# Softmax of 33.55 MB on one core: ten loads and thirteen stores of mixed size become eight and eight of 16 rows per partition

## Chip, cores, metric

One core of a Trainium2 chip; the other cores are idle. The metric is the device time of one launch in microseconds (us), median over several runs. The profile's span is about 1.9 us shorter than the time. The ratios compare runs in the fast state alone; the granted clock is 1.0.

## The reference

```python
x = np.random.randn(16, 1024, 512).astype(np.float32)      # 16,384 rows of 512
x_max = np.max(x, axis=-1, keepdims=True)
exp_x = np.exp(x - x_max)
return exp_x / np.sum(exp_x, axis=-1, keepdims=True)
```

33.55 MB are read and 33.55 MB written.

## The kernel before

The rows are cut into chunks. A chunk of R rows per partition is one load (128 x R x 2 KB), is worked on in place in groups of at most 8 rows, and is stored from the same place. The program's buffer in SBUF holds 96 rows per partition, so the last chunks take the place of the first ones and wait for those stores.

```python
CHUNKS = [                      # (rows per partition, first row in SBUF)
    (3, 0), (5, 3), (8, 8), (16, 16), (16, 32), (16, 48), (16, 64), (16, 80), (16, 0), (16, 16),
]
EARLY = 8                       # loads issued at once
AFTER_STORE = {2: [8], 3: [9]}  # load 8 after the store of chunk 2, ...
GROUP = 8
FINISH_BEFORE = (1, 2, 3)       # finish the waiting group before these chunks are begun
STORE_ROWS = {3: 8, 4: 8, 5: 8} # these chunks are stored in halves of 8 rows
ON_VECTOR = 3                   # the last three groups are scaled on VectorE
AT_HEAD = {mybir.EngineType.SP: 3}   # three loads go ahead of the entry barrier
...
def rowmax(g):   # VectorE: minus the maximum of 8 rows, one instruction
def exps(g):     # ScalarE: per row exp(x + shift), with its sum
def scale(g):    # VectorE reciprocal; GpSimd multiplies 8 rows (or VectorE, row by row)
    ...
    if since is not None:
        nc.scalar.dma_start(out=dst[k][:, since:b, :], in_=place[k][:, since:b, :])
    if b == CHUNKS[k][0]:
        for later in AFTER_STORE.get(k, ()):
            load(later)
...
for k in range(EARLY):
    load(k)                     # nc.sync.dma_start
for g, (k, a, _, _) in enumerate(groups):
    if waiting is not None and a == 0 and k in FINISH_BEFORE:
        scale(waiting); waiting = None
    rowmax(g); exps(g)
    if waiting is not None:
        scale(waiting)
    waiting = g
scale(waiting)
```

Loads are issued from SyncE, stores from ScalarE: two queues on the same 16 DMA engines.

## Time and profile before

| | before |
|---|---|
| time, median of 6 runs beside the changed kernel | 161.51 us (161.40 to 161.61) |
| span of the profiled run | 159.6 us |
| DMA packets of data per engine (packet records) | 184 |

The part of the profile that the prediction does not show is the list of DMA issues: out<-in, the issuing queue, how many, KB each, and the median time in us from issue to landing.

```profile
held<-in_x_dram SPq DMA_DIRECT2D x7, 4096.0 KB, 39.1
out_dram<-held ACTq DMA_DIRECT2D x4, 4096.0 KB, 29.1
out_dram<-held ACTq DMA_DIRECT2D x7, 2048.0 KB, 37.9
held<-in_x_dram SPq DMA_DIRECT2D x1, 768.0 KB, 4.4
out_dram<-held ACTq DMA_DIRECT2D x1, 768.0 KB, 15.8
```

The first load of 768 KB lands after 4.4 us; later a load of 4 MB, which takes 9.7 us when alone, lands 39 us after its issue (the median). A transfer that lands late here is mostly one that was queued early.

"Packet records" below are the trace's rows of single DMA packets: queue, start, duration, size. A packet is what one partition moves in one transfer (16 rows: 32 KB). The page prints only their sums; the numbers from them are worked out here, and say so. The records don't name the DMA engine; it follows from the times, since each packet starts where another of the same engine ends.

### The profile page before, as it was taken

To read this page: it belongs to the slowest core of one execution; us is meant where nothing else is said; L and a number is where in the kernel's file an instruction comes from. 1 tells how busy PE (TensorE), PEld (TensorE's weight loads), DVE (VectorE), ACT (ScalarE), POOL (GpSimd) and SP (SyncE) were. 2 spreads that over 40 slices of the span, in tenths; PEclk is the share of its full clock that TensorE was granted. 3 is DMA by queue.
4 is the path that set the end of the run, shared out by engine and by line. 5 is a ranking of instruction groups with operands and counts; after the bars stand their busy time and mean duration, and the time that the engine had idled before them with its cause. 6 is when DMAs were issued, how large, how long until landed. Compare 5 with 4: busy or idle time off the path is not lost.

```text
span 159.6 us, 442 instructions
## 1 busy us (share of the span) xinstructions
DVE 82.6 (52%) x58; ACT 92.9 (58%) x257; POOL 91.2 (57%) x18
## 2 busy tenths in 40 slices
DVE  0470903980966567393856768386479935000000
ACT  0719076039949796976979957993995760000000
POOL 0060912950899999999999999999930000000000
DMA  7999999999999999999999999989999999999994
GB/s 271 439 464 398 431 391 435 458 408 421 431 423 431 427 415 443 411 468 423 431 456 411 437 423 431 464 378 448 406 468 443 445 411 419 476 411 419 468 419 172
DMA packets 3315, 67.13 MB, mean 421 GB/s; under 512 B 368, under 2 KB 368, under 8 KB 624
## 3 DMA queue, kind: packets, MB, share of 16 engines
q1 hardware_dynamic: 1440, 33.56, 49.6%
q10 hardware_dynamic: 1872, 33.56, 49.0%
q14 instruction: 3, 0.02, 0.0%
HBM read 33.55 MB, written 33.55 MB: 420 GB/s over the span
## 4 chain that ended last, share of the span: by engine, by line
POOL 51%; issue 12%; ACT 11%; DVE 7%; DMA 3%; ACTq 0%; DVEq 0%; POOLq 0%
POOL held L150 51%; ACT held L135 11%; DVE held L157 4%; DMA held<-in_x_dram 3%; DVE shift L127 3%; ACTq L163 0%; DVE recip L147 0%; DVEq L209 0%; POOLq L150 0%; DVEq L147 0%; ACTq L135 0%
## 5 line engine op out<-in xcount | busy, mean ns | idle before, releaser
L135 ACT ACTIVATE held<-held,shift 128x512 f32<-128x512 f32 x128 | 90.4, 708 | 33.0 <-POOL held L150 29.9
L150 POOL TENSOR_TENSOR held<-held,recip 128x4096 f32<-128x4096 f32 (+2 forms) x14 | 91.0, 6529 | 25.8 <-DVE recip L147 25.8
L127 DVE TENSOR_REDUCE shift<-held 128x8 f32<-128x4096 f32 (+2 forms) x17 | 70.3, 4139 | 5.4 <-DMA held<-in_x_dram 5.4
L147 DVE RECIPROCAL recip<-sums 128x8 f32<-128x8 f32 (+2 forms) x17 | 3.4, 200 | 45.9 <-ACT held L135 45.9
L135 ACT ACTIVATION_READ_ACCUMULATOR held<-held,shift 128x1 f32 x128 | 24.0, 187 | 0.0
L157 DVE TENSOR_SCALAR held<-held,recip 128x512 f32<-128x512 f32 x24 | 10.0, 491 | 0.1
L135 ACT ACT_TABLE_LOAD x1 | 1.3, 1283 | 4.5 <-DMA held<-in_x_dram 4.5
L198 POOL MEMSET const-float32-0.0<- 128x1 f32 x1 | 0.1, 98 | 0.2 <-issue 0.2
L198 POOL MEMSET const-bfloat16-1.0<- 128x1 bf16 x1 | 0.1, 101 | 0.0
L198 POOL MEMSET const-uint8-127<- 128x1 uint8 x1 | 0.1, 101 | 0.0
L198 POOL MEMSET const-float32-1.0<- 128x1 f32 x1 | 0.1, 98 | 0.0
## 6 DMA issues: line engine op xcount, KB each, us to landing
held<-in_x_dram SPq DMA_DIRECT2D x7, 4096.0 KB, 39.1
out_dram<-held ACTq DMA_DIRECT2D x4, 4096.0 KB, 29.1
out_dram<-held ACTq DMA_DIRECT2D x7, 2048.0 KB, 37.9
held<-in_x_dram SPq DMA_DIRECT2D x1, 2048.0 KB, 11.5
held<-in_x_dram SPq DMA_DIRECT2D x1, 1280.0 KB, 7.1
out_dram<-held ACTq DMA_DIRECT2D x1, 1280.0 KB, 20.5
held<-in_x_dram SPq DMA_DIRECT2D x1, 768.0 KB, 4.4
out_dram<-held ACTq DMA_DIRECT2D x1, 768.0 KB, 15.8
```

The lines of the kernel that those rows point to most:

```text
L127: nc.vector.reduce_max(out=shift[g], in_=place[k][:, a:b, :], axis=AX, negate=True)
L135: nc.scalar.activation(out=place[k][:, r, :], in_=place[k][:, r, :], func=EXP, bias=shift[g][:, r - a : r - a + 1], scale=1.0, accum_out=s ...
L147: nc.vector.reciprocal(out=recip, in_=sums[g])
L150: nc.gpsimd.tensor_tensor(out=place[k][:, a:b, :], in0=place[k][:, a:b, :], in1=recip.unsqueeze(2).to_broadcast([P, b - a, d]), op=mybir.A ...
L157: nc.vector.tensor_scalar_mul(out=place[k][:, r, :], in0=place[k][:, r, :], scalar1=recip[:, r - a : r - a + 1],)
L198: nc = _bacc.Bacc("TRN2", target_bir_lowering=False, num_devices=1)
```

## The change

Its intent: fewer and larger transfers, all alike; no small ones at the opening nor in mid kernel.

```diff
-CHUNKS = [
-    (3, 0), (5, 3), (8, 8), (16, 16), (16, 32), (16, 48), (16, 64), (16, 80), (16, 0), (16, 16),
-]
+CHUNKS = [(16, 0), (16, 16), (16, 32), (16, 48), (16, 64), (16, 80), (16, 0), (16, 16)]
-EARLY = 8
-AFTER_STORE = {2: [8], 3: [9]}
+EARLY = 6
+AFTER_STORE = {0: [6], 1: [7]}
-FINISH_BEFORE = (1, 2, 3)
+FINISH_BEFORE = ()
-STORE_ROWS = {3: 8, 4: 8, 5: 8}
+STORE_ROWS = {}
```

## The prediction

> **What bounds the kernel now.** I read the page from the top: the engines' shares, then the DMA rows of the slices, then the DMA queues, then a table of stretches, and only then the chain and the groups.
>
> ```profile
> span 159.6 us, 442 instructions
> DVE 82.6 (52%) x58; ACT 92.9 (58%) x257; POOL 91.2 (57%) x18
> DMA  7999999999999999999999999989999999999994
> GB/s 271 439 464 398 431 391 435 458 408 421 431 423 431 427 415 443 411 468 423 431 456 411 437 423 431 464 378 448 406 468 443 445 411 419 476 411 419 468 419 172
> DMA packets 3315, 67.13 MB, mean 421 GB/s; under 512 B 368, under 2 KB 368, under 8 KB 624
> q1 hardware_dynamic: 1440, 33.56, 49.6%
> q10 hardware_dynamic: 1872, 33.56, 49.0%
> ```
>
> No compute engine is busy for more than 58% of the span. The 16 DMA engines are: the DMA row is 9 everywhere but in the first and the last slice, and the loads (q1) and stores (q10) together fill 49.6 + 49.0 = 98.6% of the engines' time. The 67.1 MB are fixed by the task (33.55 in, 33.55 out). So the time is the bytes over the rate, plus the ends. The stretches show where the rate is less than it can be:
>
> ```profile
> 0.00:2.00 2.00, 0.00 (x0) 0.00 (x0) 0.20 (x4) 1.00 0.48 135
> 2.00:12.00 10.00, 4.64 (x3) 3.52 (x8) 2.75 (x1) 1.00 1.05 445
> 12.00:22.00 10.00, 4.48 (x2) 4.77 (x13) 4.46 (x1) 1.00 0.99 405
> 22.00:32.00 10.00, 5.38 (x3) 4.59 (x14) 5.09 (x1) 1.00 1.02 436
> 32.00:42.00 10.00, 5.26 (x3) 7.60 (x21) 3.46 (x2) 1.00 1.01 422
> 42.00:106.00 64.00, 42.25 (x19) 53.21 (x151) 64.00 (x10) 1.00 1.00 430
> 108.00:157.00 49.00, 19.50 (x30) 17.23 (x50) 9.21 (x2) 1.00 1.01 434
> 157.00:159.60 2.60, 0.00 (x0) 0.00 (x0) 0.00 (x0) 1.00 0.12 50
> ```
>
> The last two columns are DMA share and GB/s; a packet is counted whole where it starts or ends, so short stretches swing by some per cent. Stores alone (108 to 157) run at 434 GB/s, the mix (42 to 106) at 430, and the only stretches below are the first 2 us and those from 12 to 42 us, at 405 and 422, with the DMA share still 0.99 and 1.01: there packets are slow, not absent. The chain and the groups:
>
> ```profile
> POOL 51%; issue 12%; ACT 11%; DVE 7%; DMA 3%; ACTq 0%; DVEq 0%; POOLq 0%
> ...
> 131.60 2.38 DVE held L157 x6
> ```
>
> ```profile
> L135 ACT ACTIVATE held<-held,shift 128x512 f32<-128x512 f32 x128 | 90.4, 708 | 33.0 <-POOL held L150 29.9 <-DVE shift L127 3.0
> L150 POOL TENSOR_TENSOR held<-held,recip 128x4096 f32<-128x4096 f32 x12 | 83.8, 7017 | 13.1 <-DVE recip L147 13.1
> L127 DVE TENSOR_REDUCE shift<-held 128x8 f32<-128x4096 f32 x15 | 65.7, 4388 | 1.0 <-DMA held<-in_x_dram 1.0
> ```
>
> The chain gives POOL 51% of the span, which misleads: it follows instructions, and its last one ends at 134.0 us, 25 us before the span does. Those 25 us are stores still queued. POOL's cadence is a margin to be checked, not the bound.
>
> **What the Trainium skill says.** (1) "DMA: Bandwidth & Descriptors", section "Where 436 GB/s comes from", puts the ceiling of the 16 engines at 435.2 GB/s. The trace agrees: 434 with stores alone. (2) The same page, section "Queues, rings and completion order", says that an engine takes turns between its queue rows, one packet at a time. The trace agrees: between 44 and 48 us, with load packets of 32 KB and store packets of 16 KB, the packet records give 282 GB/s of loads and 150 of stores, about 2 to 1. (3) The same page, section "Why small descriptors are slow (HBM only)", names a fixed cost per packet. The packet records agree: the usual packet of 6,144 bytes takes 234 ns, 16,384 take 611 and 32,768 take 1,213; a line through the first and last has an intercept of 8 ns and 27.2 bytes per ns, and gives 610 ns for the middle one. (4) "Perfetto Trace Analysis", [...]says that splitting transfers can help where DMA engines are generally idle. Here they are not, so I expect the opening's small transfers to buy no bandwidth.
>
> **The change part by part.** Ten loads (3, 5, 8 and seven of 16 rows) become eight of 16; thirteen stores (3, 5, 8, six of 8 rows and four of 16) become eight of 16. All loads but the last two are issued at once; load 6 waits for store 0, load 7 for store 1. Compute is the same per row but for two POOL calls fewer. What follows is an estimate from the durations above.
>
> *Fixed cost.* Each engine moves 8 packets per transfer: 80 + 104 = 184 packets before, 64 + 64 = 128 after. 56 packets at 8 ns are 0.45 us, and 7 completion descriptors of 9 ns are 0.06: **0.5 us gained**, on the path, as every engine is full.
>
> *The slow stretches.* The packet records between 12 and 42 us hold some 90 load packets that take 25 to 320 ns over 1,213, all of 32 KB, while store packets of 6, 10 and 16 KB come in between; summed and divided by 16 engines this is 0.8 us. After 42 us there is hardly one. I can't tell whether the small stores cause it, which go, or the 32 KB loads themselves early on, which stay. I count half: **0.4 us gained**.
>
> *Opening.* First bytes move at 1.0 us in both, since the first load is issued at 0.0. The first packets of before carry 0.3 us per engine above their size; with 32 KB packets I allow **0.1 us more**. What the small first load bought, the first reduction at 4.4 us, is gone: the first 4.19 MB land at about 12.3 us (in before the three small loads, the same bytes: issued at 0.9 and 11.5 to landing).
>
> *Does DMA go idle later?* From 12.3: reduce to 16.7 and 21.1 (4.39 each), exponentials of 8 rows 5.7 each to 22.5 and 28.2, POOL 7.0 each to 29.8 and 36.8, so store 0 is issued at 36.9, where before had sent three. Until then loads fill the engines alone, and six loads last for 25.2 / 0.431 = 58 us. Its first packet follows some 2 to 3 us later (before: issued 11.5, first packet 15.2), about 39, when 16 MB are in. From then on packets are equal and each queue gets 216 GB/s, 19.4 us per transfer. Stores 0 to 3 land at 59, 78, 98, 117; loads 4 to 7 at 62, 81, 101, 120. Load 6 is released at 59 and not due until 81; load 7 at 78 and 101: 22 us to spare each. Stores are issued at 51, 65, 79 and 93 (two POOL calls, 13.95 apart in before's chain), faster than 19.4, so the store queue never runs dry in between.
>
> *The end.* Load 7 lands at about 121. At 120, 17.5 of 33.55 MB are stored; the queue holds the rest of store 4 and store 5 (issued about 113.5, as the reciprocal of its second half stands behind the reduction that waits for load 6), 7.6 MB or 17.5 us: dry at 137.5. Store 6 stands behind the reduction of load 7's first half: 121 + 4.4 + 0.2 + 3.5 of scaling = 129, after exponentials 132: 5.5 us spare. Store 7: the second reduction ends near 133, exponentials 139, reciprocal and scaling 3.5, so 143, and the queue is dry at 147: 4 us spare. So the DMA engines stay full and the last transfer is again 4 MB.
>
> Sum: -0.5 - 0.4 + 0.1 = -0.8: 161.5 - 0.8 = **160.7 us**.
>
> **Rivals.** (a) *The late start costs.* If the kernel were bound by compute, first arithmetic 7.9 us later (12.3 for 4.4) and POOL's later start would push the end by up to 8 us: 165 to 170. For it: the chain is POOL; against: the DMA row of 9s and the 25 us of queued stores at the end. (b) *Store 6 or 7 comes late.* My spare is 4 to 5.5 us at the end, the smallest of the schedule; if loads 6 and 7 land later than at equal shares, each us beyond the spare is added: 162 to 164. Against: in before, loads land as the shares say. (c) *The slow load packets are of the opening with 32 KB loads*, and a longer time of loads alone makes more of them: at 415 GB/s instead of 431 for 37 us, 1.4 us lost: 162. For it: all slow packets are 32 KB loads; against: 22 to 26 us, nearly loads alone, ran at 430. (d) *All slow packets go*: another 0.4 gained, 160.3, the least that I see, since 67.1 MB at 433 are 155.0 us, and with 1.0 ahead, 0.5 for first packets, 1.0 behind and the 1.9 us between span and time, 159.4 is the floor.
>
> **Range and chances.** Between (d) and (c): 160.1 to 162.1. Faster by 2% would be 158.3, below that floor: 0.01. Slower by 2% would be 164.7 and needs (a) or a failed (b): 0.04. Within 2%: 0.95.
>
> **What would show it.** DMA row of 9s throughout, with the first store at about 37 us; packets down by about 1,000; load 6 issued near 59, load 7 near 78; last load landing at 120 instead of 109; last DVE scaling at about 143 instead of 134; DVE's and ACT's idle at the start up by 8 us without moving the end. A wrong prediction shows as a slice below 9 near 137 or 147 us (b), a low GB/s with full share before 40 us (c), or DMA idle before 59 us (a load that waits where I see none).

## The result

| | before | after |
|---|---|---|
| time, median of 6 | 161.51 us | 161.90 us (161.74 to 162.38) |
| span of the profiled run | 159.6 us | 159.9 us |
| ratio of fast runs, 95% interval | | 1.0028 (1.0013 to 1.0044) |

A ratio is the mean time of one kernel's fast runs over that of the other's of the same rounds, so not quite the ratio of the medians. By the 2% rule the two are the same; the difference of 0.4 us is small but outside the noise, and it has the other sign than forecast.

The same parts of the page after:

```profile
span 159.9 us, 418 instructions
DVE 82.0 (51%) x56; ACT 92.7 (58%) x257; POOL 91.0 (57%) x17
DMA  7999999999899999999999999999999999999994
GB/s 270 459 451 393 459 451 402 434 467 410 338 410 426 426 451 402 418 484 402 418 484 410 418 467 420 393 443 475 393 418 492 402 418 477 410 410 443 451 410 189
DMA packets 2307, 67.13 MB, mean 420 GB/s; under 512 B 256, under 2 KB 256, under 8 KB 256
q1 hardware_dynamic: 1152, 33.55, 49.6%
q10 hardware_dynamic: 1152, 33.55, 48.7%
```

A thousand records fewer, and the DMA engines are as full as before. In the GB/s row one slice stands out: the eleventh, 40 to 44 us, at 338. The stretches (the last two columns are DMA share and GB/s):

```profile
0.00:2.00 2.00, 0.00 (x0) 0.00 (x0) 0.20 (x4) 1.00 0.90 262
22.00:32.00 10.00, 8.36 (x4) 10.00 (x29) 9.22 (x2) 1.00 1.02 439
32.00:42.00 10.00, 5.12 (x3) 6.51 (x19) 10.00 (x2) 1.00 1.01 390
42.00:106.00 64.00, 35.36 (x16) 46.63 (x132) 57.57 (x9) 1.00 1.00 432
120.00:157.00 37.00, 18.94 (x29) 11.76 (x34) 1.06 (x1) 1.00 1.01 436
```

Before had 405 and 422 GB/s from 12 to 22 and from 32 to 42 us. After has, by the packet records, nothing slow from 4 us until 36 us and then one deeper hole with the share at 1.01: the engines are busy with packets that take longer. The chain of waits and the arithmetic's first and last rows:

```profile
DMA 52%; POOL 16%; DVE 10%; ACT 7%; issue 4%; DVEq 0%; SPq 0%
...
12.26 8.75 DVE L125 TENSOR_REDUCE shift<-held 128x8 f32<-128x4096 f32 x2 [12.26 <-DMA held<-in_x_dram]
...
140.10 3.26 DVE L155 TENSOR_SCALAR held<-held,recip 128x512 f32<-128x512 f32 x8
```

The arithmetic starts 7.8 us later (12.26 for 4.43) and ends 9.4 us later (143.4 for 134.0), and the end of the kernel moves by 0.3. The chain now says DMA 52% where it said POOL 51%, at almost the same time: it names what the last instruction waited for, not what the time is made of.

Now the ledger, from the packet records. An undisturbed packet takes 8 ns plus its bytes at 27.2 per ns (the line of the prediction, by the durations of the records). "Opening" is what packets that start before 4 us take over that, summed and divided by 16 engines; "slow" is the same for all later packets that are more than 10 ns over. The last two columns are when the last store lands, on average over the engines and on the last of them.

| us | packets per engine | opening | slow, loads | slow, stores | last landing, mean | last landing |
|---|---|---|---|---|---|---|
| before | 184 | 0.36 | 0.95 | 0.03 | 157.85 | 158.58 |
| after | 128 | 0.61 | 1.08 | 0.24 | 158.16 | 158.91 |

### The profile page after: what moved, and what is told of

Same layout as the page of the kernel before. It is cut to its first block, busy times and chain, and to the rows that moved or that the text cites. A ratio compares the mean times of both kernels' runs of the same rounds, so it can differ in the third digit from the quotient of the medians.

```text
span 159.9 us, 418 instructions
## 1 busy us (share of the span) xinstructions
DVE 82.0 (51%) x56; ACT 92.7 (58%) x257; POOL 91.0 (57%) x17
## 4 chain that ended last, share of the span: by engine, by line
DMA 52%; POOL 16%; DVE 10%; ACT 7%; issue 4%; DVEq 0%; SPq 0%
DMA held<-in_x_dram 32%; DMA out_dram<-held 20%; POOL held L148 16%; ACT held L133 7%; DVE shift L125 6%; DVE held L155 4%; DVE recip L145 0%; DVEq L207 0%; SPq L120 0%; DVEq L145 0%; DVEq L125 0%
## 5 line engine op out<-in xcount | busy, mean ns | idle before, releaser
L148 POOL TENSOR_TENSOR held<-held,recip 128x4096 f32<-128x4096 f32 x13 | 90.8, 7016 | 29.8 <-DVE recip L145 29.8
L125 DVE TENSOR_REDUCE shift<-held 128x8 f32<-128x4096 f32 x16 | 70.2, 4392 | 36.6 <-DMA held<-in_x_dram 36.6
L145 DVE RECIPROCAL recip<-sums 128x8 f32<-128x8 f32 x16 | 3.2, 200 | 24.7 <-ACT held L133 24.7
L133 ACT ACT_TABLE_LOAD x1 | 1.3, 1283 | 12.3 <-DMA held<-in_x_dram 12.3
```

The costliest lines, as they stand in the source:

```text
L125: nc.vector.reduce_max(out=shift[g], in_=place[k][:, a:b, :], axis=AX, negate=True)
L133: nc.scalar.activation(out=place[k][:, r, :], in_=place[k][:, r, :], func=EXP, bias=shift[g][:, r - a : r - a + 1], scale=1.0, accum_out=s ...
L145: nc.vector.reciprocal(out=recip, in_=sums[g])
L148: nc.gpsimd.tensor_tensor(out=place[k][:, a:b, :], in0=place[k][:, a:b, :], in1=recip.unsqueeze(2).to_broadcast([P, b - a, d]), op=mybir.A ...
```

## The experiments

The theories after reading the result. **O**: a store stream that joins a long stream of loads stalls the engines once, by about 1 us, so what before lost in pieces after loses at one place. **Rivals**: the burst falls there by chance; it is proportional to the store's packet size (P); it is the first write being cold (W); it is 16 engines in step getting in each other's way (L). Fourteen kernels ran, in five batches and not all on the same chip; the kernel before, run beside each batch, took 161.45 to 161.55 us. All gave correct results. Each kernel has one profile.

### The changed kernel again

> The changed kernel itself, for its scatter and for a second look at the stall. Theory O (onset): the engines stall once, when the first store comes into a stream of loads alone; between 36 and 44 us the load packets again carry about 1.1 us per engine over 1,213 ns, the opening again 0.6 us, and the time is 161.7 to 162.1. Rival C (chance): the burst of slow packets falls anywhere; this profile has it at another place or not at all, and the time scatters between 161.0 and 162.4.

Measured: 161.84 us, ratio 1.0057 (1.0012 to 1.0102); two of six runs took 163.6 and 163.7. The burst is at the same place: slow packets 1.06 us per engine between 36 and 40 us, 1.19 in all, opening 0.69. Chance falls. In the stretch from 36 to 44 us, the changed kernel first, then its repeat:

```profile
36.00:44.00 8.00, 3.27 (x3) 6.78 (x19) 8.00 (x3) 1.00 1.01 378
```

```profile
36.00:44.00 8.00, 3.27 (x3) 6.66 (x19) 8.00 (x3) 1.00 0.95 353
```

The single packets show it best: between 39 and 42.7 us every engine has a load packet of 1.9 to 2.6 us instead of 1.21, the last or last but one before its first store packet, and about half of them a second one of 1.3 to 1.7 us. The two runs of 163.6 stay unexplained (no profile fell on one).

### Small loads at the opening alone

```diff
-        queue.dma_start(out=place[k], in_=src[k])
+        edges = [0, *LOAD_CUTS.get(k, ()), CHUNKS[k][0]]      # LOAD_CUTS = {0: (3, 8)}
+        for a, b in zip(edges, edges[1:]):
+            queue.dma_start(out=place[k][:, a:b, :], in_=src[k][:, a:b, :])
```

> Changed kernel, but the first chunk is loaded in three pieces of 3, 5 and 8 rows; stores and groups as in the changed kernel. Ledger: the opening loses 0.6 us instead of 0.87 (first packets of 6 KB instead of 32 KB), 16 more packets of 8 ns take 0.13 of it back within that; the first store is issued about 5 us sooner (32 us) and the stall of about 1 us moves with it. Time 161.6, 0.3 under the changed kernel. Rival: the small opening is worth more (1 us, if compute's start mattered): 160.9.

Measured: 161.88 us, ratio 1.0016 (1.0002 to 1.0030). Store 0 comes about 3 us sooner, and the burst with it (nearly all of it from 34.9 to 39.3 us, 0.74 us per engine). The sooner start of the arithmetic is worth nothing that can be seen. The first 4.19 MB land at 11.73 us on average, against 11.42 in before (whose three small chunks are each contiguous) and 11.55 in the changed kernel: cut this way, the small opening is no gain.

### Store 0 in halves

```diff
-STORE_ROWS = {}
+STORE_ROWS = {0: 8}
```

> Changed kernel, but chunk 0 is stored in two halves of 8 rows (16 KB packets instead of 32 KB at the first store, issued 7 us sooner, at about 30 us). Theory O: the stall comes 7 us sooner and is as large, 1.1 us: 161.9. Rival P (packet size): the stall is in proportion to the store's packets at the first mixing, so it halves to 0.5 and the time is 161.4.

Measured: 162.04 us, ratio 1.0028 (1.0003 to 1.0052). The burst at the first store comes about 6 us sooner and is half as large (0.48 us between 28 and 40 us), as P says. But a second one of 0.47 comes at 81 to 85 us, and 0.12 at 100; the sum is 1.25. In this run smaller store packets cut the loss into pieces and did not take it away. Before's pieces at 12 to 20 and 32 to 40 us look alike, but that they have the same cause is not shown. Nor is P settled: three of the six runs took 161.45 to 161.74 us, close to the 161.4 of P, and three 162.34 to 162.61; the profile fell on one of these (162.51). And no first store explains the second loss: stores of 32 KB packets had been running since 62.7 us.

### A tiny store first

```diff
+        if g == 0:
+            nc.scalar.dma_start(out=dst[0][0:16, 0:1, :], in_=place[0][0:16, 0:1, :])
```

> Changed kernel plus one store of 16 partitions x 1 row (32 KB in all, one 2 KB packet per engine) at about 30 us; the full first store follows at about 37 and writes these rows again. Rival W (first write is cold): the stall moves to about 31 us and is gone at 39 us. Theory O: the tiny store costs 0.1 to 0.3 us, the stall at 39 to 42 us stays at about 1 us, time 161.9 to 162.1. Rival L (engines in step): a 2 KB packet does not take them out of step, so as O.

Measured: 161.84 us, ratio 1.0018 (1.0003 to 1.0032). No slow packet near 30 us; 0.97 us per engine at 36 to 44 us as before. W, in the form that any first write pays it, falls.

### Before with whole stores in mid kernel

```diff
-STORE_ROWS = {3: 8, 4: 8, 5: 8}
+STORE_ROWS = {}
```

> Kernel before without its half stores in mid kernel (three chunks stored in one piece of 16 rows instead of two of 8): the small opening stays. Fixed cost: 24 packets per engine fewer, 0.2 us gained; slow packets from 12 to 42 us as in before (0.8 us), perhaps 0.1 more where the first 32 KB store comes. Time 161.3. Rival P (32 KB store packets bring the stall of 1 us whenever they first come): 162.0.

Measured: 161.81 us, ratio 1.0022 (1.0010 to 1.0034): this part of the change alone makes the kernel before slower, by nearly as much as the whole change does. 24 packets per engine fewer should have gained 0.2 us; the last store lands on average at 157.86, before at 157.85. Slow packets are 1.10 against 0.99, the opening 0.35 against 0.36, so slow packets gave back 0.1 of the 0.2 us. The other 0.1 was not there, since a packet costs about 5 ns and not 8 (shown below, with the quarter loads). The last engine ends 1.0 us after the mean instead of 0.7, which is 0.3 of the 0.5 us that its span is longer (160.1).

### Loads in quarters

```diff
+LOAD_CUTS = {k: (4, 8, 12) for k in range(1, 8)}
```

> Changed kernel with loads 1 to 7 cut into four pieces of 4 rows: packets of 8 KB in place of 32 KB, 168 more per engine and 21 more completion descriptors. At 8 ns a packet, theory F (fixed cost per packet is on the path) says +1.5 us: 163.4 if the stall at the first store is unchanged. Rival: the fixed cost hides under the other direction's packets while both run, so only loads alone pay: +0.4, 162.3. Loads of 8 KB also lose their share of the engines beside 32 KB stores; if load 7 then lands over 4 us later, idle DMA at the end adds to it.

Measured: 173.89 us, ratio 1.0676 (1.0616 to 1.0737; two of the four runs count as slow, the ratio is from the other two, 171.16 and 173.64). Far more than both, and for the reason named last in the expectation:

```profile
14.00:34.00 20.00, 16.24 (x8) 17.02 (x48) 11.18 (x2) 1.00 1.01 424
...
150.00:157.00 7.00, 4.45 (x13) 5.75 (x16) 0.00 (x0) 1.00 0.02 9
```

The first line is the fixed cost: loads of 8 KB alone run at 424 GB/s where loads of 32 KB run at 433 by the records. Until 21.5 us a piece of 8 packets lands every 2.453 us, four of them 9.81 against 9.68 for a whole load of the changed kernel: 24 packets and 3 completion descriptors cost 0.13 us, about 5 ns a packet. After that a piece takes 2.484 us, because many of the single packets take 311 to 321 ns instead of 309; why is not shown.

Why 5 ns, where the line through the durations has 8? The records of two packets in a row on one engine overlap by 3 to 4 ns. From start to start, undisturbed packets of 32, 16 and 8 KB are 1,209, 607 and 306 ns apart, where their records last 1,213, 611 and 309. That is about 5 ns plus the bytes at 27.2 per ns, and a completion descriptor adds about 6. It is the same for loads alone (12 to 33 us in the changed kernel), for stores alone (118 to 132 us in before) and for the mix (66 to 84 us in both).

The second line is an idle DMA: beside 32 KB stores the 8 KB loads get a fifth of the bytes, the last piece lands at 145 us instead of 121, and nothing is moved from 151.5 to 160.7 us: store 7 is issued only at 159.9. The time of this kernel is swamped by that; only its loads alone are evidence for the fixed cost.

### Store 0 behind the loads, store 1 held

```diff
-            nc.scalar.dma_start(...)                     # store k, when chunk k is done
+            late = [1, 2] if k == 2 else [k] if k != 1 else []
+            for c in late:
+                queue = nc.sync if c == 0 else nc.scalar
+                queue.dma_start(out=dst[c], in_=place[c])
```

> Changed kernel, but store 0 goes on the queue of the loads, behind load 5, so that the first store starts when the early loads have ended (about 58 us) and not among them; store 1 is held until just before store 2 (about 65 us). Theory O (a store stream that joins a load stream stalls the engines once): no burst of slow load packets between 36 and 44 us, slow packets 0.1 to 0.4 us per engine in all instead of 1.2 to 1.3, time 160.8 to 161.1. Rival J (any joining of the two directions costs it): load 6, which joins the stores at about 70 us, brings the burst of 1 us there, time 161.8. Rival C (chance or time): the burst comes near 38 us with loads alone.

Measured: 165.59 us, ratio 1.0262 (1.0231 to 1.0293). The construction was flawed: store 1 waited only for its own chunk and was issued at 52 us, while load 5 was still running, and load 7 came so late that the DMA engines were idle near the end. What it still shows:

```profile
54.00:58.00 4.00, 2.85 (x3) 2.56 (x8) 4.00 (x2) 1.00 0.92 319
...
148.00:152.00 4.00, 3.46 (x9) 0.26 (x2) 0.00 (x0) 1.00 0.02 8
```

No burst at 36 to 44 us; it moved to the load packets that start from 53.8 to 56 us, just before where now the first store comes (0.86 us). It follows the first store and not the clock. And where load 6 joins running stores (88 us) there is none: rival J falls.

### Engines put out of step

```diff
         load(k)
+        if k == 1:
+            nc.sync.dma_start(out=place[5][0:8], in_=src[0][0:8])      # needless, 8 partitions
```

> Changed kernel plus one needless load of 8 partitions x 16 rows (overwritten later by load 5) behind load 1: if it is spread over 8 of the 16 engines, it puts these one packet (1.2 us) behind the others before the first store comes, half a cycle of load and store packets. Rival L (the stall is that of 16 engines in step): the burst at 36 to 44 us falls from 1.1 us per engine to under 0.5; the added bytes cost 0.6 us on average and 1.2 on the engines that carry them, so the time is 162.2 to 162.6. Theory O: the burst stays at 1.0 to 1.1, time 162.8 to 163.2.

Measured: 165.85 us, ratio 1.0271 (1.0258 to 1.0284). The stretches from 20 us and the one of the first store:

```profile
20.00:24.00 4.00, 1.90 (x3) 4.00 (x13) 1.11 (x1) 1.00 1.19 229
24.00:28.00 4.00, 3.83 (x1) 4.00 (x11) 4.00 (x1) 1.00 0.79 254
...
36.00:44.00 8.00, 5.30 (x3) 6.67 (x19) 8.00 (x3) 1.00 0.96 411
```

The burst at the first store is gone (411 against 378 and 353 GB/s; one packet is slow, by 0.4 us). But the needless 262 KB cost every engine, not just eight, 3.4 us, with packets of up to 4.4 us, and a later hole of idle DMA near 150 us. So it looked like proof of L. Three more kernels took it apart.

### The same without crowding, the same bytes spread, and a smaller step

```diff
+            nc.sync.dma_start(out=place[5][0:32:4], in_=src[0][0:32:4])                  # every_fourth
+            nc.sync.dma_start(out=place[5][:, 0:1], in_=src[0][:, 0:1])                  # even_bytes
+            nc.sync.dma_start(out=place[5][0:32:4, 0:4], in_=src[0][0:32:4, 0:4])        # quarter_step
```

> As out_of_step, but the needless load goes to partitions 0, 4, 8, ... 28, so that its 8 packets of 32 KB do not crowd on the same few partitions. Theory L (what the engines lose is the time until they stand apart; one packet of difference between half of them is enough): no burst at 36 to 44 us, slow packets in all under 0.4 us per engine after the needless load, which itself lengthens 8 engines by 1.2 us; time 161.9 to 162.5. Rival O: the burst of 1.0 to 1.1 us stays and the time is 162.5 to 163.2. Rival S (the sum of slow packets is 1 us in every variant because something of that size has to be lost once): the needless load costs what the burst would have.

Measured: 163.16 us, ratio 1.0102 (1.0089 to 1.0115). The needless load itself slows no one now, half of the engines are one packet behind (load 2 lands at 30.7 to 31.3 us on eight engines and at 31.9 to 32.4 on the other eight), and the burst is there in full: 0.96 us per engine at 36 to 44 us. **L falls.**

```profile
36.00:44.00 8.00, 3.27 (x3) 6.75 (x19) 8.00 (x3) 1.00 0.97 369
```

> Control of out_of_step and every_fourth: the needless load has the same 262 KB but is spread evenly (128 partitions x 1 row), so no engine is put behind another, while load 5 waits for it as there. Theory L: the burst at 36 to 44 us stays at 1.0 to 1.1 us per engine, time 161.9 + 0.6 = 162.5. Rival Q (the burst went in out_of_step because load 5 was issued late, at 27 us, and fewer loads were queued): the burst is gone here too, 161.4 to 161.6.

Measured: 162.68 us, ratio 1.0070 (1.0056 to 1.0085). The burst is there, 0.92 us, though load 5 was issued at 22.7 us (26.8 in out_of_step, 2.6 in the changed kernel): rival Q (load 5 issued late) falls as well.

> As every_fourth with 4 rows: 8 engines are put 0.3 us behind the other 8. Theory L in its simple form (any lasting difference helps in proportion): the burst falls by about a quarter to 0.8, time 161.9. If a small difference is enough to take the engines apart: burst under 0.3, time 161.2 to 161.5, which would beat the kernel before. Theory O: burst 1.0 to 1.1, time 162.1.

Measured: 162.31 us, ratio 1.0070 (1.0033 to 1.0106), with one run at 164.4. The burst is 1.55 us, the largest of all. No step between engines helps. What the crowding did in the kernel above to remove the burst stays open.

### Phases: loads alone, stores alone, then loads join

The edit is shown against store_behind_loads:

```diff
-            late = [1, 2] if k == 2 else [k] if k != 1 else []
+            late = [2, 1] if k == 2 else [k] if k != 1 else []
```

> store_behind_loads with its flaw mended: store 0 on the queue of the loads behind load 5, and store 1 issued after store 2 (about 65 us), so that no store comes in while loads run alone; load 6 then joins running stores at about 72 us and load 7 at about 98 us. Theory O (a store that joins loads costs about 1 us, a load that joins stores costs nothing): slow packets under 0.3 us per engine in all, last load landing by 120 us, no idle DMA, time 160.8 (160.6 to 161.2), faster than the kernel before. Rival S (about 1 us of slow packets is lost once in every order): the burst comes at 59 or at 72 us, time 161.8 to 162.1.

Measured: 162.07 us (161.44 to 163.43), ratio 1.0038 (1.0007 to 1.0069). The order came out as meant: store 0 starts on the queue of the loads when load 5 ends, store 2 is issued at 64.8 us, load 6 at 75.0, and no DMA is idle.

```profile
36.00:44.00 8.00, 6.83 (x3) 8.00 (x23) 8.00 (x3) 1.00 0.96 414
```

```profile
57.00:61.00 4.00, 3.98 (x1) 0.00 (x0) 4.00 (x2) 1.00 1.06 377
```

The burst is not at 36 to 44 us any more; it is at 57 to 61 us, 0.76 us per engine, on the last two packets of load 5 just ahead of store 0's first packets, with nothing else in flight. So O is wrong in its word "joins": the loss does not need loads and stores side by side. Rival S names it more rightly: here too it comes with the first large store. It does not come again when store 2 starts the other queue, nor when loads 6 and 7 join. "Once in every order" is more than the runs show: halves_first had its second loss at 81 to 85 us.

> phases, with the first chunk loaded in three pieces of 3, 5 and 8 rows. The opening measured so far: the first 4.19 MB land at 11.42 us on average in before and at 11.55 in the changed kernel, at 11.73 with this cut of one chunk. Theory O: as phases plus 0.0 to 0.2: 160.9 to 161.1. Rival: the sooner start of the arithmetic is worth something once the stall is gone: 160.5.

Measured: 162.36 us, ratio 1.0048 (1.0031 to 1.0064). Burst 0.79 at 57 to 61 us, opening 0.48; neither start nor opening pays.

### A row stored early

```diff
             rowmax(g)
+            if g == 0:
+                nc.scalar.dma_start(out=dst[0][:, 15:16, :], in_=place[0][:, 15:16, :])
             exps(g)
```

> Changed kernel plus one store of 128 partitions x 1 row (2 KB packets, 8 per engine, 262 KB in all) of unfinished data at about 12 us, among loads alone; the true first store writes that row again later. If the loss of 1 us is bound to the first store of some size (rival S, as in phases, where it came with no load beside it): part of it, 0.2 to 0.5 us, comes at 13 to 26 us and the burst at 38 to 42 us shrinks by the same, 0.5 to 0.8 left; the sum stays at 1.0 to 1.3 us per engine, time 162.5 (161.9 + 0.6 for the bytes). If each first meeting of a long load stream with 32 KB stores costs the full amount: 1.0 to 1.1 at 38 to 42 us all the same, time 162.6 to 162.9.

Measured: 162.51 us, ratio 1.0064 (1.0047 to 1.0081), which is the changed kernel plus the 0.6 us of the added bytes. The 2 KB packets ran from 16.4 to 25.7 us with no slow load packet beside them; the burst at 38 to 42 us is 0.80. A small store does not pay it in advance, beyond perhaps a fifth.

### The slow packets of the kernels together

| us per engine, packet records | opening | slow | where the largest part is | last landing, mean / last | median time |
|---|---|---|---|---|---|
| before | 0.36 | 0.99 | 12 to 20 us: 0.45; 32 to 40: 0.32 | 157.85 / 158.58 | 161.51 |
| whole_mid | 0.35 | 1.10 | 12 to 20: 0.44; 32 to 40: 0.34 | 157.86 / 158.88 | 161.81 |
| after | 0.61 | 1.32 | 36 to 44: 1.06 | 158.16 / 158.91 | 161.90 |
| after_again | 0.69 | 1.19 | 36 to 44: 1.09 | 158.03 / 158.80 | 161.84 |
| small_loads | 0.54 | 0.91 | 32 to 40: 0.74 | 157.87 / 158.83 | 161.88 |
| halves_first | 0.79 | 1.25 | 28 to 40: 0.48; 80 to 84: 0.47 | 158.23 / 159.59 | 162.04 |
| tiny_first | 0.65 | 1.21 | 36 to 44: 0.97 | 158.12 / 158.94 | 161.84 |
| phases | 0.66 | 0.96 | 56 to 60: 0.76 | 157.82 / 158.52 | 162.07 |
| phases_small | 0.48 | 1.04 | 56 to 60: 0.79 | 157.97 / 159.71 | 162.36 |

The row of phases belongs to its fastest run (161.44 us), the one that was profiled; its median is 0.6 higher. Left out are the kernels with added bytes or idle DMA; their slow packets sum to 1.04 us (store_behind_loads), 3.56 (out_of_step), 1.08 (every_fourth), 0.99 (even_bytes), 1.62 (quarter_step), 0.86 (early_row) and 1.35 (quarter_loads). No version beat the kernel before.

## Why the prediction was right or wrong

**Right, by its own steps.** The kernel is bound by the DMA engines and stays so; the late start costs nothing (rival a). The queue schedule held: first reduction 12.26 us (12.3 predicted), store 0 issued at 36.8 (36.9), store 5 at 114.1 (113.5), store 6 at 129.7 (132), store 7 at 143.4 (143), last load landed at 121 (121); loads 6 and 7 were released at 62.7 and 82.0, some 4 us later than the 59 and 78 predicted, out of 22 us to spare. Most of that is a misread delay: store 0's first packet was put 2 to 3 us after its issue, at 39, although the example beside it (11.5 to 15.2) says 3.7; it came at 41.4. No slice is idle at 137 or 147 us (rival b). Time within 2% and inside the range, which is partly luck: three of its terms erred, all in the same direction, and the range was wide enough. Three slips cost nothing: two POOL calls fewer were counted, it is one (14 to 13 by the page); the stretch "from 12 to 42" holds 22 to 32 us at 436, which is not slow; and the sentence of point (4) stands in that page's section "DMA Optimizations".

**Wrong: the sign.** -0.8 us was forecast and +0.4 came. Three terms of the sum failed.

*"The slow stretches ... I count half: 0.4 us gained" failed, and it is the largest.* It took the small stores as a possible cause, with a coin's chance, and so took the loss to go with them. It did not go: with 32 KB stores a loss of that size comes in one burst at the first store, and the slow packets rise from 0.99 to 1.32 and 1.19 us in the two profiles, so 0.2 to 0.3 lost for 0.4 gained. Every kernel tried has 0.9 to 1.6 us of it, but for out_of_step, which paid 3.4 us at another place. Rival (c) was near but wrong in its reason: loads alone with 32 KB packets are not slow (433 GB/s by the landings from 11.6 to 30.9 us); only the last ones before the first large store are. That the burst comes with the first large store is shown: it moved with that store in small_loads, halves_first, store_behind_loads and phases. What the engines do in that microsecond is not shown by any run. It is not chance, not a first small write and not the mixing; engines in step are ruled out by every_fourth, though why out_of_step lost the burst stays open.

*"Fixed cost ... 0.5 us gained, on the path" was too large: it is 0.3.* The prediction took the 8 ns by which a packet's record is longer than its bytes as the packet's cost on the path. The records overlap by 3 to 4 ns, so about 5 ns are on the path (quarter_loads, above), and about 6 instead of 9 for a completion descriptor: 56 packets and 7 descriptors are 0.3 us, an estimate from these spacings. Nothing of it is hidden in the mix: three rounds of one 4 MB load and one 2 MB store in before should take 14.54 us each by the spacings and take 14.56 by the landings of the stores (54.15, 68.71, 83.25, 97.83 us); rounds of 4 + 4 MB in after should take 19.36 and take 19.39 (60.45, 79.85, 99.22, 118.63 us), with 0.02 of slow packets in them.

*"Opening ... 0.1 us more" was 0.25 to 0.33 by the records.* The first 32 KB packet of each engine takes 1.4 to 2.1 us instead of 1.21. In landings, the first 4.19 MB come at 11.55 instead of 11.42 us, 0.13 later although 16 packets per engine fewer had to be moved.

Together, in place of -0.5 - 0.4 + 0.1 = -0.8: the fixed cost -0.3, slow packets +0.33 and the opening +0.25 give +0.28 us, and the mean landing of the last store moved by +0.31. In the repeat, -0.3 + 0.20 + 0.33 give +0.23, and it moved by +0.18. The rest of the +0.4 in the medians lies in the unprofiled runs, whose scatter is larger for after (161.74 to 162.38) than for before (161.40 to 161.61); its cause stays open.

## What to carry to other kernels

When the DMA engines are full from end to end, merging transfers gains only the fixed cost of a packet, read from the distance between packets and not from their durations: here about 5 ns each, 0.3 us of 161; what a late start of the arithmetic costs is read from the queue of stores left at the end. Before a lossy stretch is entered as a gain, find out whether the change removes its cause or only moves it: here one kernel with the first store put elsewhere would have told. And an experiment that seems to prove a cause needs its control: the load to eight crowded partitions removed the burst, the same load to eight spread ones did not.

## What the Trainium skill lacked or had wrong

- No page says that load packets just ahead of the first large store are slow, by about 1 us per engine: 1.06 and 1.09 us at 36 to 44 us in the two profiles of the changed kernel (0.8 to 1.55 in variants), 0.76 at 57 to 61 us where the store followed the loads on one queue; 2 KB store packets did not trigger it.
- "DMA: Bandwidth & Descriptors", section "Latency and other measured facts", gives about 600 ns to the first byte for this path and does not say from where. Here the first packet starts 0.99 to 1.03 us after the issuing instruction begins and 0.62 to 0.66 us after it ends; counted from its end, the figure agrees. It does not say that the first packets of 32 KB then take 1.4 to 2.1 us instead of 1.21.
- No page says that the records of successive packets on one engine overlap (3 to 4 ns here), so that a packet's duration overstates its fixed cost on the path: 8 ns by the durations, about 5 by the distance from start to start.
- "SBUF — State Buffer", section "Door 1: The DMA port swizzle", puts partitions 0 to 7 on two ports, and the crowded load agrees (262 KB, slow packets from 20.5 to 28.4 us, against none when spread over partitions 0, 4, ... 28). It does not say that the other engines' packets to other partitions are held up too: all 16 engines lost 3.4 us each. The skill tells of such back-pressure only for DMA between cores.
